# Low parts of the MLP weights from an adding DMA instead of VectorE, in a float32 two-layer trunk

## The chip, the cores and the metric

The kernel runs on one core of one Trainium2 chip. The metric is the device time of one execution, in microseconds. A core has TensorE (PE, matmuls; PEld is its weight load), VectorE (DVE), ScalarE (ACT), GpSimd (POOL), SyncE (SP) and 16 DMA engines that all queues share.

## The reference

One sequence of 256 tokens with 2048 features goes through two layers, each with attention, a layer norm, an MLP of 8192 hidden features and another layer norm. The change touches the MLPs alone:

```
def sq_relu_mlp(x, w1, w2):
    return jnp.square(jax.nn.relu(x @ w1)) @ w2
...
h = layer_norm(ALPHA * h + mix, ln1_g[layer], ln1_b[layer])
h = layer_norm(ALPHA * h + sq_relu_mlp(h, mlp_w1[layer], mlp_w2[layer]), ln2_g[layer], ln2_b[layer])
```

Layer 0 has a causal attention with forget gates, layer 1 an attention over compressed, selected and windowed keys. All inputs are float32; `w1` is 2048 x 8192 and `w2` 8192 x 2048 a layer.

## The kernel before

Every large product is made from float32r parts: a float32 operand x is split into a high part (x rounded to float32r) and a low part (x minus high), and a product takes three of the four combinations: high x high, high x low, low x high.

Weights come in blocks of 128 partitions x 1024 float32, 512 KB, "half k" of a block of weights. `wload` makes one ready: a load into one of 4 `raw` buffers, issued on SP's DMA queue, then `fill_split`, in which ScalarE rounds `raw` to the high half of a `whl` tile (L117) and VectorE subtracts the high half from `raw` into the low half of the tile (L118). There are 5 `whl` buffers. ScalarE can start when a `whl` buffer has been released by the matmuls that read it and the load has landed; the `raw` buffer comes free when VectorE is done, and the SP queue then issues the load of the block four later. The queues of all engines work in order.

`mlp(layer, acts, ln)` goes through the hidden features in four quarters of 2048. In a quarter, the w1 stage (`ws_stream`, `ws_many`) takes 16 slices of 128 columns of w1, each in two halves of 8 row blocks. A row block kt needs two matmuls: a wide one with the high weights against both halves of the activations (L151, 512 columns) and a low one with the low weights against the high activations (L152, 256 columns). So a half has 16 matmuls. In the first quarter the first three slices run together. Each finished slice is merged (ScalarE L185, VectorE L187), squared behind its relu (VectorE L385) and split into an activation chunk. The w2 stage (`out_proj`, `xs_part`, `xs_mm`) takes 512 output columns at a time (index n) over four parts kc of 512 hidden features, each part in two halves of the weights (index k); a half has 12 matmuls of 512 columns (L173): per row block and 128 tokens high x high, high activations x low weights, low x high. The last quarter leaves its last 512 columns to `end`, which calls `wload` itself and overlaps the layer norm.

GpSimd issues a few DMAs in the attention layers: four of 512 KB into the tile `bc`, four into `nbm`, one of 2 MB into `b_dram`, and small ones. In the MLPs it has nothing to do until the last layer norm. `warm` is a run of matmuls without use, put into the norms.

Of the kernel before, what the change touches and what calls it, by code (L numbers as in the profile page):

```python
# [52 lines left out]
def constants():  # L53
    """Identity, triangles, stacked identities and masks: they depend on shapes alone."""
    i = np.arange(P)
    eye = np.eye(P, dtype=np.float32)
    upper = (i[:, None] <= i[None, :]).astype(np.float32)
    causal = np.where(i[None, :] > i[:, None], np.float32(BIG), np.float32(0))

    def stacked(n):  # L60
        a = np.zeros((P, n), np.float32)
        a[np.arange(2 * n), np.arange(2 * n) % n] = 1
        return a

    t = np.arange(S).reshape(2, P)
    d_c = t[:, :, None] - (16 * np.arange(NC) + 31)
    keep = (d_c >= 0).astype(np.float32).transpose(1, 0, 2).reshape(P, 2 * NC)
    cst = [eye, upper, np.ones((P, P), np.float32), np.zeros((P, P), np.float32), causal,
           stacked(60), stacked(48), stacked(16), keep]

    def onehot(*dists):
        """Block k of 32 rows picks the bucket of distance k; row 96 + k says that the key lies ahead."""
        a = np.zeros((99, len(dists[0])), np.float32)
        c = np.arange(len(dists[0]))
        for k, dist in enumerate(dists):
            ok = dist >= 0
            a[NB * k + buckets(dist)[ok], c[ok]] = -1
            a[96 + k, c[~ok]] = 1
        return a

    oh = [onehot(255 - np.arange(384))]
    for tb in range(2):
        oh += [onehot(*(d_c[tb, :, n + k] for k in range(3))) for n in range(0, NC, 3)]
    ahead = np.zeros((99, 3, H), np.float32)
    ahead[[96, 97, 98], [0, 1, 2]] = BIG
    oh.append(ahead.reshape(99, 3 * H))
    return np.ascontiguousarray(np.concatenate(cst, 1)), np.ascontiguousarray(np.concatenate(oh, 1))
# [11 lines left out]
def _trunk(nc, tc, i, out, ctx):  # L99
# [23 lines left out]
    def wload(src, k, pool=wp, bufs=5, pieces=1):  # L123
        """Half k of a block of weights, split."""
        raw = raw_tile()
        w = pool.tile([P, 2, HALF], F32R, tag="whl", name="whl", bufs=bufs)
        n = HALF // pieces
        for s in (slice(a, a + n) for a in range(0, HALF, n)):
            load(raw[:, s], src[k][:, s])
            fill_split(w[:, 0, s], w[:, 1, s], raw[:, s])  # L130
        return w

# [8 lines left out]

    def ws_many(srcs, acts, accs, half=None):
        """accs = (128 columns of a matrix each)^T @ x^T, over the wide halves of x; half: rows 0-1023 or the rest."""
        for kt in range(KT) if half is None else range(8 * half, 8 * half + 8):
            if kt % 8 == 0:
                ws = [wload(src, kt // 8) for src in srcs]
            a = acts[kt // 4][:, kt % 4]
            s = slice(kt % 8 * P, (kt % 8 + 1) * P)
            last = kt == KT - 1
            for w, acc in zip(ws, accs):  # L150
                wide = lambda: mm(acc, w[:, 0, s], a, start=kt == 0, stop=last)  # L151
                low = lambda: mm(acc[:, :S], w[:, 1, s], a[:, 0, :], start=False, stop=False)  # L152
                if last:
                    low(), wide()
                else:
                    wide(), low()

    def ws_stream(srcs, acts, use, together=1):
        """Each of srcs is one 128-column slice of a matrix; use(j, acc) gets its product, transposed."""
        j = 0  # L160
        while j < len(srcs):
            n = together if j == 0 else 1
            accs = [acc_tile() for _ in range(n)]
            ws_many(srcs[j:j + n], acts, accs)
            for k, acc in enumerate(accs):
                use(j + k, acc)
            j += n
# [6 lines left out]

    def xs_part(src, act, accs, first, last, pieces=1):
        """accs[t] += (512 columns of x)[tokens t] @ 512 x 512 of a matrix"""
        ws = [wload(src, k, pieces=pieces if k == 0 else 1) for k in range(2)]
        for kt in range(4):
            for t in range(2):
                xs_mm(accs[t], act, kt, t, ws[kt // 2], first and kt == 0, last and kt == 3)  # L180

    def merge(dst, acc, scale=1.0):
        """dst = scale * (the wide product's two halves)"""
        t = sp.tile([P, S], F32, tag="mt", name="mt")
# [6 lines left out]
    def narrow(src, n, acts, st, dst):  # L191
        """dst[:, tok, :] = x @ (2048 x n) for a small n; returns its last step."""
        raw = wp.tile([P, KT, n], F32, tag="raw", name="nraw", bufs=4)
# [31 lines left out]

    def out_proj(src, acts, first, ln=None, two=False, between=()):
        """h = (ALPHA h or h) + acts @ W, 512 columns at a time (two: the first 1024 at once).

        between's steps come after the parts. With ln, the last 512 columns are left to what it returns,
        which ends with the layer norm."""  # L230
        between = list(between)
# [13 lines left out]
        def one(n, accs, kcs):  # L245
            for kc in kcs:
                xs_part(src[n, kc], acts[kc], accs[n], kc == 0, kc == 3)
                step()
# [19 lines left out]
        def end(late, meanwhile=None):  # L268
            """Tokens 128-255 come behind, so that the norm of the others overlaps with their products."""
            ln.gains(late)  # L270
# [30 lines left out]
    class Norm:  # L301
        """Layer norm of h in place, in pieces of 128 tokens x 512 features, with what use does to a piece."""

# [55 lines left out]
    def transposer(cs):  # L359
        """Puts the pieces into cs, transposed and split, in chunks of 512 features."""  # L360
        def use(t, c):
# [14 lines left out]
    def mlp(layer, acts, ln):  # L376
        for q in range(4):
# [9 lines left out]

            ws_stream([i["w1"][layer, q * 16 + j] for j in range(16)], acts, use, 3 if q == 0 else 1)
            end = out_proj(i["w2"][layer, q], hid, q == 0, ln if q == 3 else None)
        with tc.tile_pool(name="late", bufs=2) as late:  # L390
            end(late)

    # ---- attention: the steps that both kinds share
    def exp_rows(E, L, m, sums):
# [4 lines left out]

    # ================= layer 0: forgetting attention  # L400
    bfb = cp.tile([P, H], F32, name="bfb")
# [8 lines left out]
    def warm(n, lhs, rhs):  # L410
        """Keeps the tensor engine's clock up while it waits."""
        idle = ps_lg.tile([P, 512], F32, tag="lg", name="idle")
# [18 lines left out]
    def forget_gates():  # L431
        """Log of the forget gates."""
        f = sp.tile([P, 5, 2, H], F32, name="f", bufs=1)
# [144 lines left out]
    with tc.tile_pool(name="late", bufs=2) as late:  # L578
# [6 lines left out]
        def tables():  # L585
            """Tables of the relative bias, negated, with BIG where a key lies ahead"""
            r_ps = ps_lg.tile([P, 512], F32, tag="lg", name="rps")
# [17 lines left out]

    # ================= layer 1: sparse attention over keys and values of layer 0's output
    with tc.tile_pool(name="np", bufs=2) as np_:
# [4 lines left out]
        gate = np_.tile([P, 2, 3 * H], F32, name="gate", bufs=1)  # L612
        # keys of the two branches and of the compressed blocks, split: per group, high and low parts of
        # [selected 0-127, window 0-127, compressed, selected 128-255, window 128-255]
        kT = np_.tile([P, G, 2, KW], F32R, name="kT", bufs=1)
        kcT = np_.tile([P, G, NC], F32, name="kcT", bufs=1)
        vhl = np_.tile([P, 2, 2, 512], F32R, name="vhl", bufs=1)
        v1 = np_.tile([P, 2, 512], F32, name="v1", bufs=1)
        # compressed values in three bands of rows (high, high, low parts), to meet high, low and high weights
        vc = np_.tile([BAND, G, P], F32R, name="vc", bufs=1)  # L620
# [5 lines left out]
        def bands(t):  # L626
            """The three bands of the columns of t"""
            return bass.AP(tensor=t.tensor, offset=t.offset, ap=[*[list(x) for x in t.ap[:-1]], [32, 3], [1, NC]])
# [46 lines left out]
        def compress(s):  # L675
            """First product of the compression; returns its later steps."""
            acc = acc_tile()
# [180 lines left out]
def laid_out(a):  # L858
    """The inputs in the order in which the kernel reads them."""
    def cols(w):  # L860
        # 128 columns of all rows, in two halves of the rows: [n, half, p, (kt c)]
        k, n = w.shape
        return w.reshape(2, k // P // 2, P, n // P, P).transpose(3, 0, 2, 1, 4).reshape(n // P, 2, P, HALF)

    def rows(w):
        # 512 columns of 512 rows, in two halves of the rows: [n, kc, half, p, (kt c)]
        k, n = w.shape
# [53 lines left out]
```

## Time and profile before

| | |
|---|---|
| time, median of 2 runs | 2260.77 us (2259.89 to 2261.65) |
| span of the profiled execution, first to last instruction | 2258.3 us |
| around that span, against the median | 2.5 us |
| mean granted TensorE clock | 0.995 of full speed |
| TensorE busy | 2233.2 us, 99% |
| VectorE busy | 1406.5 us, 62% |
| ScalarE busy | 1047.0 us, 46% |
| GpSimd busy | 18.5 us, 1% |
| DMA, all queues | 427.54 MB, mean 189 GB/s |
| SP's queue | 419.00 MB, 56.9% of 16 engines' time |

Busy time does not count the issue of DMAs, and a busy TensorE is not one at its peak, because its matmuls are pipelined. The share of DMA is the time that packets took on the 16 engines. An engine's idle time matters only where the chain of work that ended last goes through it.

### The profile page before, as it was taken

What the parts mean: (1) busy time and instruction counts of PE and PEld (TensorE: products, weight loads), DVE (VectorE), ACT (ScalarE), POOL (GpSimd) and SP (SyncE); (2) the same over time, 40 slices, a digit from 0 to 9 for tenths busy, and PEclk for the clock granted to TensorE, in tenths of its full rate; (3) what the DMA queues carried; (4) which work ended last, traced back from release to release, by engine and by line L of the source; (5) the groups of instructions that cost most, each with busy time, mean ns of one, the idle gap of its engine ahead of it and who ended that gap; (6) DMA issues with size and microseconds to landing.
All of it is one profiled execution on the core that took longest, in us unless ns stands there. A gap on an engine that the chain in (4) does not pass through costs nothing.

```text
span 2258.3 us, 30147 instructions
## 1 busy us (share of the span) xinstructions
PE 2233.2 (99%) x11478; PEld 1890.7 (84%) x11478; DVE 1406.5 (62%) x2209; ACT 1047.0 (46%) x1564; POOL 18.5 (1%) x26
## 2 busy tenths in 40 slices
PE   9999999999999999999999999999999999999997
PEld 7888888888888888888788888888888888888885
DVE  6565556764565565565786688667655645655655
ACT  5444444443444444444355567544434434444442
POOL 0000000000000000000000000000000000000001
PEclk9999999999999999999999999999999999999998
DMA  7665557556555555555556744565565566565563
GB/s 252 197 206 180 173 197 243 195 187 191 191 186 192 192 187 191 191 187 190 183 170 211 252 134 133 171 212 177 187 194 188 187 194 189 186 195 188 187 194 113
DMA packets 116829, 427.54 MB, mean 189 GB/s; under 512 B 13179, under 2 KB 13339, under 8 KB 115406
## 3 DMA queue, kind: packets, MB, share of 16 engines
q1 hardware_dynamic: 114734, 419.00, 56.9%
q0 software_dynamic: 1952, 6.63, 1.0%
q8 instruction: 90, 1.47, 0.3%
q14 instruction: 53, 0.43, 0.1%
HBM read 423.45 MB, written 4.24 MB: 189 GB/s over the span
## 4 chain that ended last, share of the span: by engine, by line
PE 97%; DVE 2%; DMA 1%; ACT 0%; issue 0%; SPq 0%; DVEq 0%
PE acc L173 44%; PE acc L151 31%; PE acc L152 16%; PE acc L683 1%; PE pt L367 1%; PE pt L830 1%; PE pt L808 0%; PE lg L766 0%; DMA bc<-c_dram 0%; DVE h L354 0%; PE acc L199 0%; PE pt L831 0%; PE pt L524 0%; PE lg L491 0%; PE lg L762 0%; DVE h L339 0%
## 5 line engine op out<-in xcount | busy, mean ns | idle before, releaser
L118 DVE TENSOR_TENSOR whl<-raw,whl 128x1024 fp32r<-128x1024 f32 (+1 forms) x769 | 937.9, 1223 | 617.9 <-ACT whl L117 608.5
L117 ACT CAST whl<-raw 128x1024 fp32r<-128x1024 f32 (+1 forms) x769 | 804.5, 1049 | 740.4 <-PE acc L173 489.6
L151 PE MATMUL acc<-act,whl 128*128 128x512 f32 x3072 | 1089.5, 401 | 0.0
L173 PE MATMUL acc<-whl,act 128*128 128x512 f32 x4416 | 1011.7, 390 | 1.0 <-DVE whl L118 1.0
L173 PEld LDWEIGHTS acc<-whl,act 128*128 128x128 f32 x4416 | 827.6, 188 | 175.4 <-DVE whl L118 1.8
L152 PE MATMUL acc<-act,whl 128*128 128x256 f32 x3072 | 834.3, 282 | 0.0
L151 PEld LDWEIGHTS acc<-act,whl 128*128 128x128 f32 x3072 | 569.7, 189 | 124.1 <-issue 0.2
L152 PEld LDWEIGHTS acc<-act,whl 128*128 128x128 f32 x3072 | 581.4, 189 | 16.7
L185 ACT ACTIVATE mt<-acc 128x256 f32<-128x256 f32 x192 | 73.3, 382 | 308.6 <-PE acc L151 308.6
L187 DVE TENSOR_TENSOR mu<-acc,mt 128x256 f32<-128x256 f32 x128 | 54.1, 424 | 120.3 <-ACT mt L185 120.3
L385 DVE SCALAR_TENSOR_TENSOR mu<-mu 128x256 f32<-128x256 f32 x128 | 54.2, 425 | 4.2
L117 ACT CAST act<-mu 128x256 fp32r<-128x256 f32 x128 | 52.0, 408 | 4.3 <-DVE mu L385 2.6
L118 DVE TENSOR_TENSOR act<-mu,act 128x256 fp32r<-128x256 f32 x128 | 53.4, 419 | 0.0
L117 ACT CAST act<-pt 128x256 fp32r<-128x256 f32 x80 | 29.5, 372 | 43.8 <-PE pt L367 32.7
L241 DVE TENSOR_TENSOR h<-h,acc 128x512 f32<-128x512 f32 x48 | 30.8, 681 | 13.2 <-PE acc L173 13.2
L118 DVE TENSOR_TENSOR act<-pt,act 128x256 fp32r<-128x256 f32 x80 | 33.0, 419 | 9.2 <-ACT act L117 9.0
L395 ACT ACTIVATE E<-E,sm 128x128 f32<-128x128 f32 (+1 forms) x64 | 29.0, 453 | 7.7 <-DVE sm L398 7.4
L354 DVE SCALAR_TENSOR_TENSOR h<-h,mv,lnb 128x256 f32<-128x256 f32 (+1 forms) x53 | 26.5, 541 | 0.1
L395 ACT ACTIVATE E<-L,sm 128x128 f32<-128x128 f32 (+1 forms) x32 | 14.3, 449 | 25.3 <-DVE sm L398 25.3
L367 PE MATMUL pt<-cst,h 128*128 128x128 f32 x96 | 18.8, 294 | 6.3 <-DVE h L354 6.0
L339 DVE SCALAR_TENSOR_TENSOR h<-h,mv,lng 128x256 f32<-128x256 f32 (+1 forms) x53 | 25.0, 501 | 0.0
L239 DVE SCALAR_TENSOR_TENSOR h<-h,acc 128x512 f32<-128x512 f32 x32 | 20.6, 680 | 4.5 <-PE acc L173 4.5
(173 smaller groups left out, 664.9 us busy)
## 6 DMA issues: line engine op xcount, KB each, us to landing
raw<-in_w SPq DMA_DIRECT2D x512, 512.0 KB, 3.5
raw<-in_fq SPq DMA_DIRECT2D x32, 512.0 KB, 3.6
raw<-in_fk SPq DMA_DIRECT2D x32, 512.0 KB, 3.5
raw<-in_fo SPq DMA_DIRECT2D x32, 512.0 KB, 3.6
raw<-in_kvT SPq DMA_DIRECT2D x32, 512.0 KB, 4.4
raw<-in_nq SPq DMA_DIRECT2D x32, 512.0 KB, 3.6
raw<-in_no SPq DMA_DIRECT2D x32, 512.0 KB, 3.6
raw<-in_fv SPq DMA_DIRECT2D x31, 512.0 KB, 3.5
```

The lines of the kernel that those rows point to most:

```text
L117: nc.scalar.copy(hi, src)
L118: nc.vector.tensor_sub(lo, src, hi.bitcast(F32))
L151: wide = lambda: mm(acc, w[:, 0, s], a, start=kt == 0, stop=last)
L152: low = lambda: mm(acc[:, :S], w[:, 1, s], a[:, 0, :], start=False, stop=False)
L173: mm(acc, l, w[:, r, s], start=first and n == 0, stop=last and n == 2)
L185: nc.scalar.activation(t, acc[:, S:], AF.Copy, scale=scale)
L187: nc.vector.tensor_add(dst, acc[:, :S], t)
L241: nc.vector.tensor_add(hcols(t, n), hcols(t, n), acc)
L354: nc.vector.scalar_tensor_tensor(hs, hs, rstd, b, op0=OP.mult, op1=OP.add)
L367: nc.tensor.transpose(tp[:, k * P:(k + 1) * P], h[:, t, f:f + P], eye)
L385: nc.vector.scalar_tensor_tensor(u, u, 0.0, u, op0=OP.max, op1=OP.mult)
L395: nc.scalar.activation(E, L, AF.Exp, bias=m, scale=-1.0, accum_out=sums)
```

## The change

A new function `wload_added` makes some of the blocks ready in another way. ScalarE writes the high half as before, and then, in a second pass over `raw`, the negated rounded value into the low half; a DMA issued by GpSimd adds `raw` onto that low half in place, which leaves raw minus high. VectorE has no part in it. The source of the adding DMA is the `raw` buffer (`far` False) or once more the weights in DRAM (`far` True).

In w1 it is used for the second half (kt 8 to 15) of each slice, except for the slices that run together; the source is `raw`. In w2 it is used for the second half of the parts kc 1 and 3, except in `end`; the source is DRAM. The other blocks, the attention layers and the numbers of buffers stay as they are. (The docstrings and comments that the diff also takes out are left out here.)

```diff
+    def wload_added(src, k, far):
+
+        raw = raw_tile()
+        w = wp.tile([P, 2, HALF], F32R, tag="whl", name="whl", bufs=5)
+        load(raw, src[k])
+        nc.scalar.copy(w[:, 0, :], raw)
+        nc.scalar.mul(w[:, 1, :], raw, -1.0)
+        nc.gpsimd.dma_start(w[:, 1, :], src[k] if far else raw, accum_op=OP.add)
+        return w
+
...
-    def ws_many(srcs, acts, accs, half=None):
+    def ws_many(srcs, acts, accs, half=None, added=False):
...
-                ws = [wload(src, kt // 8) for src in srcs]
+                ws = [wload_added(src, 1, False) if added and kt else wload(src, kt // 8) for src in srcs]
...
-    def ws_stream(srcs, acts, use, together=1):
+    def ws_stream(srcs, acts, use, together=1, added=False):
...
-            ws_many(srcs[j:j + n], acts, accs)
+            ws_many(srcs[j:j + n], acts, accs, added=added and j >= together)
...
-    def xs_part(src, act, accs, first, last, pieces=1):
+    def xs_part(src, act, accs, first, last, pieces=1, added=False):
...
-        ws = [wload(src, k, pieces=pieces if k == 0 else 1) for k in range(2)]
+        ws = [wload_added(src, k, True) if added and k else wload(src, k, pieces=pieces if k == 0 else 1) for k in range(2)]
...
-    def out_proj(src, acts, first, ln=None, two=False, between=()):
+    def out_proj(src, acts, first, ln=None, two=False, between=(), added=False):
...
-                xs_part(src[n, kc], acts[kc], accs[n], kc == 0, kc == 3)
+                xs_part(src[n, kc], acts[kc], accs[n], kc == 0, kc == 3, added=added and kc % 2 == 1)
...
-            ws_stream([i["w1"][layer, q * 16 + j] for j in range(16)], acts, use, 3 if q == 0 else 1)
-            end = out_proj(i["w2"][layer, q], hid, q == 0, ln if q == 3 else None)
+            ws_stream([i["w1"][layer, q * 16 + j] for j in range(16)], acts, use, 3 if q == 0 else 1, True)
+            end = out_proj(i["w2"][layer, q], hid, q == 0, ln if q == 3 else None, added=True)
```

## Rows read from the trace of the kernel before

**Rows 1.** The page, its parts 1 and 4: busy time and share of the span of each engine, and the shares of the chain of work that ended last.

```profile
PE 2233.2 (99%) x11478; PEld 1890.7 (84%) x11478; DVE 1406.5 (62%) x2209; ACT 1047.0 (46%) x1564; POOL 18.5 (1%) x26
...
PE 97%; DVE 2%; DMA 1%; ACT 0%; issue 0%; SPq 0%; DVEq 0%
```

**Rows 2.** The page, its part 5, groups by line over the whole run: line, engine, operation, out<-in, count | busy us, mean ns of one | idle us of the engine just before them, and who ended most of it.

```profile
L118 DVE TENSOR_TENSOR whl<-raw,whl 128x1024 fp32r<-128x1024 f32 (+1 forms) x769 | 937.9, 1223 | 617.9 <-ACT whl L117 608.5
...
L117 ACT CAST whl<-raw 128x1024 fp32r<-128x1024 f32 (+1 forms) x769 | 804.5, 1049 | 740.4 <-PE acc L173 489.6
...
L151 PE MATMUL acc<-act,whl 128*128 128x512 f32 x3072 | 1089.5, 401 | 0.0
...
L173 PE MATMUL acc<-whl,act 128*128 128x512 f32 x4416 | 1011.7, 390 | 1.0 <-DVE whl L118 1.0
```

**Rows 3.** Busy time by windows, core 0, a w2 stage (677 to 766 us) and a w1 stage (766 to 854 us) of the first MLP.

```profile
core 0: us, PE busy (x) PEld busy (x) DVE busy (x) ACT busy (x) POOL busy (x), PEclk, DMA share, GB/s
677.00:766.00 89.00, 89.00 (x397) 73.82 (x396) 45.67 (x44) 35.39 (x35) 0.00 (x0) 1.00 0.60 193
766.00:854.00 88.00, 88.00 (x500) 76.31 (x499) 55.97 (x77) 42.82 (x62) 0.00 (x0) 1.00 0.58 186
```

**Rows 4.** The timeline of ScalarE in a w1 stage: start us, duration us, engine, line, operation, out<-in, count [idle before <- releaser].

```profile
596.06 1.05 ACT L117 CAST whl<-raw 128x1024 fp32r<-128x1024 f32 x1 [1.12 <-PE acc L152]
598.85 0.38 ACT L185 ACTIVATE mt<-acc 128x256 f32<-128x256 f32 x1 [1.74 <-PE acc L151]
599.13 1.04 ACT L117 CAST whl<-raw 128x1024 fp32r<-128x1024 f32 x1
600.18 0.41 ACT L117 CAST act<-mu 128x256 fp32r<-128x256 f32 x1
601.71 1.05 ACT L117 CAST whl<-raw 128x1024 fp32r<-128x1024 f32 x1 [1.12 <-PE acc L152]
...
607.36 1.05 ACT L117 CAST whl<-raw 128x1024 fp32r<-128x1024 f32 x1 [1.06 <-PE acc L152]
```

**Rows 5.** Who waited for whom between 595 and 680 us (w1): us in total, times, longest.

```profile
ACT mt L185 <- PE acc L151: 27.0, 15, 1.8
...
ACT whl L117 <- PE acc L152: 16.0, 15, 1.1
```

**Rows 6.** The timelines of VectorE and of SP's DMA queue in the same stage, columns as in rows 4.

```profile
597.14 1.22 DVE L118 TENSOR_TENSOR whl<-raw,whl 128x1024 fp32r<-128x1024 f32 x1 [1.03 <-ACT whl L117]
...
598.39 0.33 SPq L114 DMA_DIRECT2D raw<-in_w  x1
```

**Rows 7.** DMA between 595 and 680 us (w1): the hardware queue (packets, MB, share of 16 engines' time), the loads (count, KB each, median us from issue to landing), and the spread of that time.

```profile
q1 hardware_dynamic: 4322, 15.74, 57.8%
...
raw<-in_w SPq DMA_DIRECT2D x30, 512.0 KB, 3.5
...
DMA to landing us min/median/max: 3.3/3.5/3.8
```

**Rows 8.** The timeline of ScalarE in a w2 stage, columns as in rows 4.

```profile
519.55 1.05 ACT L117 CAST whl<-raw 128x1024 fp32r<-128x1024 f32 x1 [1.67 <-PE acc L173]
522.27 1.06 ACT L117 CAST whl<-raw 128x1024 fp32r<-128x1024 f32 x1 [1.67 <-PE acc L173]
```

**Rows 9.** The DMAs of 512 KB that GpSimd issues in the attention layers, from DRAM into the tiles `bc` and `nbm`: duration of the issue in ns (min/median/max), first and last start, and the time from issue to landing.

```profile
L469 POOL DMA_DIRECT2D bc<-c_dram x4: 527/530/559, 47.4 to 131.2; - x4
...
DMA to landing us min/median/max: 4.6/5.3/5.9
...
L750 POOL DMA_DIRECT2D nbm<-b_dram x4: 748/752/766, 1140.8 to 1400.7; - x4
...
DMA to landing us min/median/max: 4.1/4.2/6.0
```

**Rows 10.** The DMA issues of the whole run: the largest transfer of GpSimd, DRAM to DRAM: engine, count, KB, us from issue to landing.

```profile
b_dram<-r_dram POOLq DMA_DIRECT2D x1, 2048.0 KB, 9.7
```

**Rows 11.** DMA between 500 and 590 us (w2), the same three lines as in rows 7.

```profile
q1 hardware_dynamic: 4776, 17.36, 60.6%
...
raw<-in_w SPq DMA_DIRECT2D x34, 512.0 KB, 4.2
...
DMA to landing us min/median/max: 3.4/4.2/4.6
```

**Rows 12.** DMA between 40 and 140 us, where GpSimd's four `bc` transfers run beside loads of weights: the software queue (packets, MB, share of 16 engines' time).

```profile
q0 software_dynamic: 608, 2.11, 7.5%
```

**Rows 13.** Busy time by windows, two stretches in which TensorE waits (columns as in rows 3; PEclk is the granted clock as a share of full speed).

```profile
60.00:70.00 10.00, 8.85 (x52) 7.50 (x51) 9.07 (x22) 4.24 (x9) 0.53 (x1) 1.00 0.65 222
...
400.00:410.00 10.00, 7.21 (x36) 5.96 (x36) 8.21 (x25) 2.06 (x6) 1.32 (x2) 0.66 0.62 204
```

## The prediction

> **What bounds the kernel now.** I read the totals first, then the chain of work that ended last: TensorE is busy 99% of the span, the chain is 97% PE, and VectorE holds 2% of it [rows 1]. The groups by line say the same from the other side: over the whole run the matmuls that read weight blocks waited 1.0 us for a VectorE split, while VectorE and ScalarE sat idle in front of their splits for 618 and 740 us [rows 2]. The windows by stage confirm it for the MLPs: in a w1 and in a w2 stage PE is busy in every microsecond, VectorE about 51 to 64% [rows 3]. So the change takes work from an engine that ends nothing. What matters is how early a block of weights is ready, and the timelines tell that.
>
> The w1 pace: the splits of the odd halves start at 596.06, 601.71 and 607.36 [rows 4], so one column slice (two blocks) takes PE 5.65 us, a block 2.83 and a pair of slices 11.30. The even halves (599.13) start behind the merge. Every odd split is released by PE [rows 4, 5]: a `whl` buffer coming free starts it, its data have long been there. VectorE starts 0.03 us after ScalarE's part and ends at 598.36, and the next load into that `raw` buffer is issued at 598.39 [rows 6]; it lands 3.5 us later, at 601.9, 5.5 us before its split at 607.36 [rows 7]. That 5.5 us is the cover on which the change draws. In w2 the pace is 2.72 us a half [rows 8].
>
> **What is removed, added and moved.** In w1 the second half of each column slice is changed, except for the first three slices of a layer's first quarter: 13+16+16+16 = 61 a layer, 122 in all. In w2 it is only the second half of parts kc 1 and 3, two of eight halves: 15 column blocks x 2 = 30 a layer, 60 in all. So 182 of the 512 MLP loads are changed, 36% and not half.
>
> VectorE loses 182 x 1.223 us = 223 us [rows 2]. None of it was on the path: worth 0. ScalarE gets a second pass over `raw`: I price it like the first, 1.05 us, 191 us in all. In w1 it starts where ScalarE now sits idle for 1.74 us ahead of the merge [rows 4], in w2 in a gap of 1.67 us [rows 8]: it costs no ScalarE queueing, only delay of the block. Without that gap the merge and the next split behind it would come up to 1.05 us later.
>
> GpSimd gets 182 DMA issues; one of 512 KB holds its queue 0.53 to 0.75 us [rows 9]. Nothing else is queued there inside the MLPs. The SP queue has as many loads as before, but in w1 a load into an odd `raw` buffer now waits for the add to land, not for VectorE, because the add reads `raw`; all later loads stand behind it in SP's order. In w2 the add reads DRAM again, so `raw` comes free after ScalarE's second pass, at about the time of today.
>
> **The add itself** is in no row, so I bound it. Call X its time from issue to landing. Plain copies of 512 KB from GpSimd's queue land in 4.1 to 6.0 us, medians 4.2 and 5.3 [rows 9]; the slowest landing from that queue, of 2 MB, is 9.7 us [rows 10]. Nearest are the 5.3 us copies, which ran beside loads. An add must fetch two operands for one result, so I add the engine time of one more plain transfer: 57.8% of 85 us over 30 loads = 1.64 us [rows 7]. X = 5.3 + 1.64 = 6.9 us, with 4.1 and 9.7 as ends. A gain is excluded, since PE waited 1.0 us for splits in all [rows 2].
>
> **w1, the raw loop.** There are 4 `raw` buffers and two blocks a slice, so two of the four buffers always hold changed halves, and each must go round in 11.30 us: two ScalarE passes 2.1, hand-overs about 0.1 (0.03 each [rows 6]), X, then the next load L. With today's L of 3.5 the loop closes if X is at most 11.3 - 5.7 = 5.6 us. With adds on the same engines L will not stay 3.5: at a DMA share of 60.6% it is already 4.2, at most 4.6 [rows 11]. I take 4.2. Loop = 2.1 + 0.1 + 6.9 + 4.2 = 13.3 us, 2.0 us more than PE needs for a pair.
>
> The engine time gives a second view. Four loads a pair take 4 x 1.64 = 6.6 us. GpSimd's copies took 7.5% of 100 us for 2.11 MB, 1.86 us per 512 KB [rows 12]; two adds at that price make 10.3 us a pair (fits), at twice that 14.0 us (2.7 us over). The loop's 13.3 lies between; it is my value.
>
> The excess must first eat the lead. An odd block gets its buffer at 596.0, its add would land at 598.2 + 6.9 = 605.1, and PE needs it four blocks after the release, at 607.3: 2.2 us in hand, regained in each w2 stage, so 8 x 2.2 = 18 us are free. w1 costs 61 pairs x 2.0 - 18 = **+104 us**.
>
> **w2.** Same reckoning: release 519.5, add landed at 519.55 + 2.2 + 6.9 = 528.7, wanted at 519.5 + 4 x 2.72 = 530.4. Cover 1.7 us: 0, as long as X stays under 8.6; beyond, 60 times the excess. Engine time for four halves: 4 x 1.60 [rows 11] + 3.72 = 10.1 of 10.9 us, just inside.
>
> The sum: the profiled execution's span of 2258.3 us and 2.5 us around it make 2260.8, the median of the two runs; +104 gives **2365 us**, +4.6%.
>
> One rule of the Trainium skill bears on X. Collectives: The Full Stack, section "The bandwidth ceiling: the fold count and why AG ≠ RS ≠ AR", has the adding transfer at half the rate of a copy because it reads two sources, the add costing nothing, with about 31 GB/s per engine for the copy. By its figures 16 engines would add 512 KB in an estimated 2.1 us and a pair would need 6.6 + 4.2 = 10.8 us, inside 11.3, which is the first rival. No run here shows an adding transfer yet.
>
> **The rivals.** *No change, the other side*: the add is little dearer than GpSimd's copies, X at most 5.6 us with L near 3.5. Then the raw loop closes in 11.3 us, PE never waits, and the time is 2261. For it: medians of 4.2 and 5.3 us [rows 9]. Against: the same rows go up to 6.0 for plain copies, and loads slow down with the share. If X ends between 5.6 and 6.6 with L at 3.5, the loss stays under 45 us (1.0 x 61, less 8 x 2.5 us of lead), also no change by what a measurement of this kernel can tell, 2%. Chance 0.24.
>
> *Much dearer adds*: X = 9.7, L = 4.6. Loop 16.5, +5.2 x 61 = 317; no lead is left, and w2 loses (9.7 - 8.6) x 60 = 66: 2644. For it: the two reads and the write of one byte range may not overlap as a copy's do; no row excludes it. TensorE's clock could add to it: the granted clock was 0.66, between 1.2 and 2.4 GHz, in a stretch with PE idle 2.8 of 10 us, but 1.00 with 1.15 of 10 idle [rows 13]; my forecast idles 2.0 of 13.3, between these. Chance 0.12.
>
> *The change doesn't do what it says*: a third of the blocks, and 191 us of the 223 us return on ScalarE. That gives 2261 too and is counted with no change. *Faster*: a less busy VectorE could shorten the norms, whose share of the chain is part of those 2%, but the change leaves their instructions alone: 0.02 over 2%.
>
> **How the numbers follow.** My forecast's mechanism holds 0.62, with 2306 to 2547 as its own range: 2306 is X = 6.6 with L = 3.5, where the loss is no longer told from none, and the top is X = 9.0 with L = 4.4 (loop 15.6, +4.3 x 61 = 262, no lead left, w2 0.4 x 60 = 24: 2547). No change reaches down to 2257. So the range is 2257 to 2547; it leaves out the dear adds and the faster case, some 0.14. Faster 0.02, same 0.24, slower 0.74.
>
> **What would show it.** Right: idle PE in the w1 stages ahead of the low matmuls (L152), released by the adding DMA; odd loads waiting for that DMA in SP's waits; landing of the add near 7 us; w1 slices at about 6.6 us in place of 5.65; w2 stages still 32 x 2.72 = 87 us; DMA share in w1 near 90%. Wrong: adds landing within 5.6 us and slices at 5.65 (no change), or waits in w2 as well (dear adds). If ScalarE's second pass is not 1.05 us, or the adds do not overlap with one another on GpSimd's queue, the loop's terms are off by that much.

## The result and the profile after

The changed kernel takes 2293.9 us, median of 2 runs (2290.3 and 2297.5), against 2260.8 before: 1.0145 times as long, interval 1.0126 to 1.0164. That is 33 us more; the prediction had 104. The time lies inside the prediction's whole range (2257 to 2547), whose lower part comes from the rival of no change, and under its mechanism's own (2306 to 2547). The profiled execution has a span of 2288.4 us, 30 us more than before.

The page of the changed kernel: busy time by engine, the DMA queues (packets, MB, share of 16 engines' time), the chain that ended last by engine, the groups by line that changed, and the DMA issues (count, KB, median us from issue to landing). Lines from 132 on stand 10 lower than before: L161 and L162 are the wide and low matmuls of w1, L183 those of w2, L138 and L139 ScalarE's two passes, L140 the adding DMA.

```profile
PE 2242.8 (98%) x11478; PEld 1893.5 (83%) x11478; DVE 1197.3 (52%) x2033; ACT 1211.7 (53%) x1740; POOL 170.1 (7%) x202
...
q1 hardware_dynamic: 114734, 419.00, 55.3%
q0 software_dynamic: 27296, 98.92, 23.0%
...
PE 83%; DMA 11%; DVE 2%; issue 2%; ACT 1%; SPq 0%; POOLq 0%; ACTq 0%; POOL 0%; DVEq 0%
...
L118 DVE TENSOR_TENSOR whl<-raw,whl 128x1024 fp32r<-128x1024 f32 (+1 forms) x593 | 722.6, 1222 | 598.4 <-ACT whl L117 592.9
...
L162 PE MATMUL acc<-act,whl 128*128 128x256 f32 x3072 | 837.8, 283 | 13.6 <-DMA whl<-raw 12.8
...
L139 ACT ACTIVATE whl<-raw 128x1024 fp32r<-128x1024 f32 x176 | 185.7, 1055 | 0.0
...
L140 POOL DMA_DIRECT2D whl<-raw x116 | 99.7, 860 | 766.8 <-ACT whl L139 471.2
L140 POOL DMA_DIRECT2D whl<-in_w x60 | 51.8, 863 | 602.4 <-ACT whl L139 551.0
...
raw<-in_w SPq DMA_DIRECT2D x512, 512.0 KB, 5.1
whl<-raw POOLq DMA_DIRECT2D x116, 512.0 KB, 6.6
whl<-in_w POOLq DMA_DIRECT2D x60, 512.0 KB, 7.9
```

VectorE lost 209 us, ScalarE gained 165, and PE now waits 12.8 us for the add from `raw` (before: 1.0 us for splits in all [rows 2]). The chain has 11% of DMA in it. So the kind of loss is the forecast one, and the add's own time is nearly the forecast one; the size is not.

A w1 stage away from the first quarter shows why that is odd. DMA between 590 and 680 us, then the timeline of ScalarE, GpSimd and SP's queue around three changed halves (the line with x6 stands for six loads, the last of which is the one at 617.16):

```profile
q1 hardware_dynamic: 4428, 16.12, 49.7%
q0 software_dynamic: 2160, 7.87, 47.3%
```

```profile
608.08 1.05 ACT L138 CAST whl<-raw 128x1024 fp32r<-128x1024 f32 x1 [1.12 <-PE acc L162]
...
613.74 1.05 ACT L138 CAST whl<-raw 128x1024 fp32r<-128x1024 f32 x1 [1.12 <-PE acc L162]
614.69 1.06 ACT L139 ACTIVATE whl<-raw 128x1024 fp32r<-128x1024 f32 x1
...
619.39 1.05 ACT L138 CAST whl<-raw 128x1024 fp32r<-128x1024 f32 x1 [0.66 <-PE acc L162]
...
610.38 0.86 POOL L140 DMA_DIRECT2D whl<-raw  x1 [4.83 <-ACT whl L139]
616.04 0.86 POOL L140 DMA_DIRECT2D whl<-raw  x1 [4.79 <-ACT whl L139]
...
601.95 15.54 SPq L114 DMA_DIRECT2D raw<-in_w  x6
...
617.16 0.33 SPq L114 DMA_DIRECT2D raw<-in_w  x1
```

The second pass ends at 615.75 and the add is issued 0.29 us later. The DMA engines are at 97% of their time, loads land in 5.1 us and adds in 6.6, so a buffer's turn is 2.0 + 0.3 + 6.6 + 5.1 = 14.0 us, longer than the forecast's 13.3. Yet the odd splits start 5.65 us apart, as before [rows 4]. Where the time went is told by the start of the first matmul of each stage, in the trace of a kernel, less that in the trace of before; the table gives what each stage added to it, in us (q0 to q3 are the quarters; the first quarters are counted from behind the norm, and the attention layers are left out).

```
                    layer 0                                layer 1
              w1q0 w2q0 w1q1 w2q1 w1q2 w2q2 w1q3 w2q3 | w1q0 w2q0 w1q1 w2q1 w1q2 w2q2 w1q3 w2q3
changed       10.9  0.9  0.0  0.1  1.9  0.0  0.0  1.2 |  9.9  0.0  1.2  0.5  2.1  0.0  0.0  0.0
e3 (turns)    18.0  5.6 12.0  5.0 13.8  3.5 14.6  6.5 | 16.6  5.0 12.3  7.4 13.9  5.9 14.0  4.2
e5 (DRAM)      7.2  0.6  1.3  0.0  0.0  0.0  0.6  0.0 |  4.1  0.7  0.0  0.0 -0.1  0.6  0.1  0.0
e6 (more raw)  7.0  0.0  0.0  0.0  0.0  0.0  0.0  4.4 |  2.6  0.0  0.0  0.0  0.0  0.0  0.0  4.1
e7 (not q0)   -0.1  0.9  1.0  0.8  0.0  0.4  0.0  0.0 |  0.0  0.0  0.0  0.0  2.7  1.3 -0.1  0.1
e8 (copy)      5.1  0.0  0.0  0.0  0.0  0.0  0.0  0.0 |  5.6  0.0  0.0  0.0  0.0  0.0  0.0  0.0
e9 (gains)     8.3  0.7  0.9  0.1  0.0  0.0  0.0  4.9 |  4.7  0.0  0.0  0.3  1.4  1.4  0.0  4.4
e12 (q0 only) 10.9  0.0  0.0  0.0  0.0  0.0  0.0  0.0 |  8.9  0.0  0.0  0.0  0.0  0.0  0.0  0.0
e13 (slice 8)  1.2  1.1  0.0  0.0  1.9  1.2  2.6  1.6 |  1.6  1.1  0.0  0.0  0.7  1.8  0.2  1.2
```

Of the 29 us by which the changed kernel's last matmul starts later, 20.8 fall in w1 of the two first quarters; in the six others w1 loses 0 to 2.1 us each. The rows e3 to e13 belong to the experiments below.

### The profile page after: what moved, and what is told of

The parts are those of the page before. It is cut to its first block, busy times and chain, and to the rows that moved or that the text cites. A ratio compares the mean times of both kernels' runs of the same rounds, so it can differ in the third digit from the quotient of the medians.

```text
span 2288.4 us, 30658 instructions
## 1 busy us (share of the span) xinstructions
PE 2242.8 (98%) x11478; PEld 1893.5 (83%) x11478; DVE 1197.3 (52%) x2033; ACT 1211.7 (53%) x1740; POOL 170.1 (7%) x202
## 4 chain that ended last, share of the span: by engine, by line
PE 83%; DMA 11%; DVE 2%; issue 2%; ACT 1%; SPq 0%; POOLq 0%; ACTq 0%; POOL 0%; DVEq 0%
PE acc L183 42%; PE acc L161 24%; PE acc L162 12%; DMA raw<-in_w 5%; DMA whl<-raw 4%; DMA whl<-in_w 1%; DVE whl L118 1%; ACT whl L117 1%; PE pt L840 1%; PE pt L818 0%; PE lg L776 0%; DMA bc<-c_dram 0%; PE pt L377 0%; DVE h L364 0%; PE acc L693 0%
## 5 line engine op out<-in xcount | busy, mean ns | idle before, releaser
L161 PE MATMUL acc<-act,whl 128*128 128x512 f32 x3072 | 1093.9, 402 | 3.1 <-ACT whl L117 3.1
L118 DVE TENSOR_TENSOR whl<-raw,whl 128x1024 fp32r<-128x1024 f32 (+1 forms) x593 | 722.6, 1222 | 598.4 <-ACT whl L117 592.9
L183 PE MATMUL acc<-whl,act 128*128 128x512 f32 x4416 | 1012.8, 390 | 3.8 <-DMA whl<-in_w 1.7
L183 PEld LDWEIGHTS acc<-whl,act 128*128 128x128 f32 x4416 | 826.9, 188 | 180.0 <-DMA whl<-in_w 3.1
L117 ACT CAST whl<-raw 128x1024 fp32r<-128x1024 f32 (+1 forms) x593 | 620.6, 1049 | 540.5 <-PE acc L183 300.9
L162 PE MATMUL acc<-act,whl 128*128 128x256 f32 x3072 | 837.8, 283 | 13.6 <-DMA whl<-raw 12.8
L161 PEld LDWEIGHTS acc<-act,whl 128*128 128x128 f32 x3072 | 571.8, 189 | 127.1 <-ACT whl L117 3.5
L162 PEld LDWEIGHTS acc<-act,whl 128*128 128x128 f32 x3072 | 583.5, 190 | 35.3 <-DMA whl<-raw 17.0
L138 ACT CAST whl<-raw 128x1024 fp32r<-128x1024 f32 x176 | 185.1, 1052 | 209.1 <-PE acc L183 96.6
L139 ACT ACTIVATE whl<-raw 128x1024 fp32r<-128x1024 f32 x176 | 185.7, 1055 | 0.0
L140 POOL DMA_DIRECT2D whl<-raw x116 | 99.7, 860 | 766.8 <-ACT whl L139 471.2
L140 POOL DMA_DIRECT2D whl<-in_w x60 | 51.8, 863 | 602.4 <-ACT whl L139 551.0
```

What stands on the lines that cost most here:

```text
L117: nc.scalar.copy(hi, src)
L118: nc.vector.tensor_sub(lo, src, hi.bitcast(F32))
L138: nc.scalar.copy(w[:, 0, :], raw)
L139: nc.scalar.mul(w[:, 1, :], raw, -1.0)
L140: nc.gpsimd.dma_start(w[:, 1, :], src[k] if far else raw, accum_op=OP.add)
L183: mm(acc, l, w[:, r, s], start=first and n == 0, stop=last and n == 2)
```

## The experiments

Theory A: the turns of the `raw` buffers decide, and the prediction had these turns wrong. The addresses in the compiled program show them: `raw` buffers are not handed round in a fixed order. In the steady w1 stages the buffer of a changed half is given out again 5 blocks later, that of a plain half 3 blocks later. The trace agrees: the half that is loaded at 601.95 has its first pass at 608.08 and its add at 610.38, and when that add has landed, at 617.1, the load at 617.16 starts, the fifth behind it. A turn then has 5 x 2.83 = 14.1 us for the 14.0 us of a changed half and 8.5 us for the 2.3 + 5.1 = 7.4 us of a plain one: it just closes. Theory B: the time of the DMA engines decides, 97% used.

**Fixed turns.** The four buffers are split in two and two, so that a changed half's buffer comes round every 4 blocks, as the prediction assumed.

```diff
-    def raw_tile():
-        return wp.tile([P, HALF], F32, tag="raw", name="raw", bufs=4)
+    def raw_tile(odd=0):
+        return wp.tile([P, HALF], F32, tag="raw%d" % odd, name="raw%d" % odd, bufs=2)
...
-        raw = raw_tile()
+        raw = raw_tile(k % 2)
```

> The changed kernel, but with the four raw buffers split into two for first halves and two for second halves of weight blocks, so that a buffer of a changed half comes round every 4 blocks as the prediction assumed (in the changed kernel it is given every 5 blocks and a plain half's every 3). Theory A (the raw buffers' turns decide): with add 6.5 us, load 5.1, two passes 2.1 and the issue 0.3 behind them a turn takes 14.0 us against 11.3, or 13.3 if the loads get quicker again; w1 slows to 6.6 to 7.0 us a slice and the kernel to about 2360 (2330 to 2400). Theory B (the DMA engines' time decides, the turns don't): as the changed kernel, 2294.

Measured 2427.5 us, 1.0746 (1.0724 to 1.0767), +167 us: above A's range, and far from B. The timeline of ScalarE in the second quarter, with the first passes of four changed halves running, PE's waits over the whole run (us, times, longest), and one line of what SP's queue waited for between 640 and 700 us:

```profile
623.13 1.05 ACT L138 CAST whl<-raw 128x1024 fp32r<-128x1024 f32 x1 [1.72 <-PE acc L162]
...
629.33 1.05 ACT L138 CAST whl<-raw 128x1024 fp32r<-128x1024 f32 x1 [1.62 <-DMA raw<-in_w]
...
637.34 1.05 ACT L138 CAST whl<-raw 128x1024 fp32r<-128x1024 f32 x1 [3.98 <-PE acc L161]
...
642.58 1.05 ACT L138 CAST whl<-raw 128x1024 fp32r<-128x1024 f32 x1 [1.60 <-DMA raw<-in_w]
```

```profile
PE acc L162 <- DMA whl<-raw: 86.0, 68, 3.4
PE acc L183 <- DMA whl<-in_w: 27.7, 9, 4.3
```

```profile
SPq L114 <- DMA whl<-raw: 26.8, 8, 5.0
```

A slice takes (642.58 - 623.13) / 3 = 6.5 us, and the w1 stages of the table lose 115 us over 116 adds, 2.0 us a pair: the prediction's own loop, in the turns it had assumed. (The compiled program of this run differs in one thing more: in w1 SP's queue loads the plain half of the next slice ahead of the changed half of this one. It waits for an add all the same, 8 times between 640 and 700 us.) w2 loses 43 us more, which the prediction had at 0; its stages follow w1 stages that have used up every lead, which is argued and not traced.

The control keeps the fixed turns and takes the adds out:

> The kernel before with the raw buffers split in two and two, no adds: the control for the fixed turns. A plain half holds its buffer 2.3 us of splitting and 3.5 to 4.2 us of loading in a turn of 11.3 us: no loss, 2258 to 2264. If it loses, the fixed turns themselves cost, not the adds in them.

2266.8 us, 1.0029 (1.0020 to 1.0039): a miss by some 3 us, but its trace loses nothing from the first MLP on. The 9 us by which it comes late are there at the start of the first MLP, in layer 0's attention. So the MLP losses of the experiment come from adds in fixed turns. (The order of loads that came with them is not in the control, whose w1 loads, but for the first ones of the first quarters, stand in the order of the source.)

**More buffers.** The changed halves of w1 get three `raw` buffers of their own, in a pool beside.

```diff
+        raw = raw_tile() if far else more[-1].tile([P, HALF], F32, tag="mraw", name="mraw", bufs=3)
```

> The changed kernel, but the changed halves of w1 load into three raw buffers of their own (a turn of 6 blocks, 17 us) beside the four of the others. The DMA work is the same. Theory A (turns of the raw buffers): the waits in the first quarter of each MLP go almost wholly, 2262 to 2272. Theory B (DMA engines at 97% in w1): no change against the changed kernel, 2290 to 2297.

2279.2 us, 1.0082 (1.0067 to 1.0097). Between the theories: 14 of the 33 us go with the DMA work unchanged, which B excludes (the order of the loads in SP's queue changed with the buffers); 19 stay, more than A said. By the table all w1 loss behind the first quarters is gone, and the first quarters still lose 7.0 and 2.6 us; there the DMA engines are nearly full. Windows of that kernel (busy us by engine, granted clock, DMA share, GB/s):

```profile
440.00:470.00 30.00, 25.52 (x133) 21.93 (x132) 11.79 (x22) 18.46 (x27) 4.27 (x5) 0.89 0.92 263
470.00:500.00 30.00, 30.00 (x171) 26.00 (x171) 13.30 (x22) 19.37 (x27) 4.30 (x5) 1.00 1.01 277
```

That full engines are what stops it there is not shown, and the second window speaks against it: at a share of 1.01 PE is busy throughout. The 4 us in the last w2 stage of each MLP are new, and were not followed up.

**Adds of w1 from DRAM.** The `raw` buffer comes free after the second pass.

```diff
-                ws = [wload_added(src, 1, False) if added and kt else wload(src, kt // 8) for src in srcs]
+                ws = [wload_added(src, 1, True) if added and kt else wload(src, kt // 8) for src in srcs]
```

> The changed kernel, but the adds of w1 also read the weights from DRAM again, so that the raw buffer comes free after ScalarE's second pass; 116 x 0.52 MB more are read from DRAM, the adds themselves are as many. Theory A (turns of the raw buffers): faster than the changed kernel, 2265 to 2280, unless adds land later than 8.7 us, where the whl buffers are late. Theory B (DMA time): the same or slower than the changed kernel, 2294 to 2310.

2275.9 us, 1.0065 (1.0048 to 1.0083), inside A's range: adds that land later (8.0 us) and move more from DRAM cost half as much, as theory A has it: they don't hold `raw`. The first quarters still lose 7.2 and 4.1 us.

**Where the adds stand.** First w1 or w2 alone, by leaving `added` off in the other stage:

> Adds in w1 alone (116), w2 as in the kernel before. Theory A: the waits of w1 stay, 2283 to 2290 (in the trace of the changed kernel w1 stages lost 10.9 + 9.9 + 1.9 + 1.2 + 2.1 us against the kernel before). Theory B (DMA time): w2 no longer takes DMA time, part of the lead is rebuilt in w2; 2275 to 2290.

> Adds in w2 alone (60, from DRAM), w1 as in the kernel before. The prediction's cover for w2 was 1.7 us with the add at 6.9 us; it landed at 7.9, still under 8.6. All theories: 2261 to 2265, at most 0.2%.

2286.3 us, 1.0115 (1.0100 to 1.0130), and 2260.6 us, 1.0001 (0.9992 to 1.0011). The adds of w1 carry the loss; those of w2 alone are free, though they land at 7.9 us: the cover reckoned for w2 holds. Beside the adds of w1 they are perhaps not free: with both, the time is 2293.9 us against 2286.3 with w1's alone, but the intervals overlap. Both theories' ranges had room for 2286. Then the first quarters:

```diff
-            ws_stream([i["w1"][layer, q * 16 + j] for j in range(16)], acts, use, 3 if q == 0 else 1, True)
+            ws_stream([i["w1"][layer, q * 16 + j] for j in range(16)], acts, use, 3 if q == 0 else 1, q > 0)
```

> The changed kernel, but w1 of the first quarter of each MLP is left as in the kernel before (26 adds fewer of 176). Theory A (the loss arises where no lead of ready blocks exists and cannot be built up, right behind a norm): 20 of the 33 us go, 2268 to 2276. Rival (each add costs its share): 33 x 26/176 = 5 us go, 2289. Theory B (DMA time) lies near the rival.

2267.7 us, 1.0030 (1.0016 to 1.0044): 26 of the 33 us go with 26 of 176 adds. And the other way round, `q == 0` and no adds in w2:

> Adds only in w1 of the first quarter of each MLP, 26 in all. Theory A: these 26 carry most of the loss, +15 to +21 us, 2276 to 2282. Rival (the adds of the quarter before leave engines or buffers behind, the loss needs all 176): 2261 to 2266.

2278.7 us, 1.0088 (1.0073 to 1.0103): these 26 adds alone cost 18 us, and by the table they cost it in the stages in which they stand.

**What is the matter with the first quarter.** Windows of 12 us in the first one, one line of the kernel before and then the changed kernel:

```profile
432.00:444.00 12.00, 12.00 (x69) 10.42 (x68) 9.74 (x14) 5.61 (x9) 0.00 (x0) 1.00 0.81 267
```

```profile
432.00:444.00 12.00, 8.06 (x34) 6.06 (x33) 3.12 (x4) 4.26 (x6) 0.85 (x1) 0.80 0.86 243
444.00:456.00 12.00, 12.00 (x64) 10.24 (x64) 5.73 (x10) 7.62 (x11) 1.70 (x2) 0.92 0.82 229
456.00:468.00 12.00, 11.79 (x68) 10.06 (x67) 5.16 (x9) 8.08 (x12) 1.71 (x2) 1.00 0.97 278
...
480.00:492.00 12.00, 10.64 (x61) 9.01 (x60) 5.45 (x9) 7.98 (x13) 1.72 (x2) 1.00 0.98 266
```

Some 25 us into the stage, where the three slices that run together are done and the changed halves begin, PE stands still for 3.9 of 12 us, and the granted clock falls to 0.80 and 0.92; then it goes on waiting a little. The chain through it is a plain half (start, us, what):

```profile
432.64 1.23 DVE whl L118
433.89 5.07 DMA raw<-in_w
439.06 1.05 ACT whl L117
440.13 1.24 DVE whl L118
```

A load is issued the moment a split frees its buffer and is wanted the moment it lands: no lead.

In layer 0 this wait has a second cause, which the compiled program shows: PE's instructions there do not stand in the order of the source. The plain halves of slices 3 to 6 come first, with a single matmul of each changed half between them, and the other 15 matmuls of each of these changed halves only behind the last plain one. So PE uses up plain halves faster than one a slice, and waits for one while work on changed halves stands behind it (two of their adds, issued at 422.22 and 431.05, have landed by 437.8). The buffers are not given out 5 and 3 blocks later there: the plain half of slice 6 gets the buffer that the plain half of slice 5 has just left, which is the chain above, and the changed half of slice 6 gets it next. PE around the wait, and its waits between 407 and 512 us:

```profile
436.61 0.40 PE L161 MATMUL acc<-act,whl 128*128 128x512 f32 x1
440.16 0.79 PE L161 MATMUL acc<-act,whl 128*128 128x512 f32 x1 [3.15 <-ACT whl L117]
...
441.80 0.63 PE L161 MATMUL acc<-act,whl 128*128 128x512 f32 x1
...
442.44 0.63 PE L161 MATMUL acc<-act,whl 128*128 128x512 f32 x1
...
450.36 0.40 PE L161 MATMUL acc<-act,whl 128*128 128x512 f32 x1
...
450.72 0.40 PE L161 MATMUL acc<-act,whl 128*128 128x512 f32 x1
```

```profile
PE acc L161 <- ACT whl L117: 3.1, 1, 3.1
PE acc L162 <- DMA whl<-raw: 2.5, 5, 1.4
```

In layer 1's first quarter (1546 to 1649 us) the program keeps the order of the source, and PE's waits are all for adds:

```profile
PE acc L162 <- DMA whl<-raw: 6.0, 4, 2.4
```

There 9.9 us are lost all the same, so the loss does not hang on that order; how much of layer 0's 10.9 us it costs was not separated.

SP's queue gave another thought. In it the load of `lng` waits 17.0 us ahead of the w1 loads (`SPq L114 <- DVE h L364: 17.0, 1, 17.0`), so I thought that this wait emptied the lead, and put the gains' loads behind the last w2 loads:

```diff
-            ln.gains(late)
+            with tc.issue_after(queue[-1]):
+                ln.gains(late)
```

> The changed kernel, but the loads of the MLP norm's gains (lng and lnb, 1 MB each) are put behind the last w2 loads in SP's order. In both kernels lng stands in SP's queue ahead of w1 loads of the first quarter and waits 17 us there for its buffer. Theory A': that wait empties the lead of ready blocks just where the changed halves begin, and the changed kernel can't rebuild it; then the first-quarter loss (10.9 + 9.9 us) falls to some 2 us each, 2268 to 2276. Rival (the norm itself or the three slices that run together at the start empty the lead): 2287 to 2294.

2287.1 us, 1.0124 (1.0106 to 1.0143), in the rival's range. That theory fell: the first quarters still lose 8.3 and 4.7 us, and the late gains cost 4.9 and 4.4 us at the ends of w2. With the `raw` buffers full, SP's loads had to wait anyway: in this run one waits 30.1 us for a VectorE split. Whether the norm or the three slices that run together empty the lead was not tried. Both edits together:

> Both edits: gains' loads later, and three raw buffers of their own for the changed halves of w1. Theory A': nearly no loss is left but for waits at the end of w2's last quarter (4 us each with more raw buffers alone), 2261 to 2270. Rival (DMA engines at 97 to 100% of their time in w1): 2276 or more.

2280.0 us, 1.0086 (1.0071 to 1.0101), as with the buffers alone, and in the rival's range. That does not show full engines to be the cause, for the reason given there.

What was left of theory A was that the lead is missing behind the norm and is not built up again. In the changed kernel four buffers give a block every (14.0 + 7.4) / 2 / 4 = 2.68 us, 0.15 us ahead of PE a block; before, every (2.3 + 3.5) / 4 = 1.45 us. So I let the changed halves begin at slice 8 of the first quarter and not at slice 3:

> The changed kernel, but in the first quarter of each MLP the changed halves begin with slice 8 in place of slice 3 (10 adds fewer of 176). Theory A: behind the norm PE has hardly a ready block in hand; with plain halves the lead is rebuilt in five slices, with changed halves it is not, since the raw buffers' turns give a block every (14.0 + 7.4)/2/4 = 2.68 us against 2.83 us that PE needs. Then most of the first-quarter loss goes, as where the whole quarter is left plain: 2267 to 2274. Rival (the first quarter is dear all along, whatever stands before the adds): 8/13 of its 21 us stay, 2283 to 2290.

2276.2 us, 1.0064 (1.0047 to 1.0081), 2 us above A's range and outside the rival's. The table is clearer: the two first quarters lose 1.2 and 1.6 us in place of 10.9 and 9.9. In layer 0 this edit also brings PE's program nearly back to the order of the source, so there two things changed; layer 1, in that order in both kernels, shows what the later start alone does. The windows of this run in the first quarter:

```profile
410.00:440.00 30.00, 29.91 (x180) 26.03 (x179) 25.06 (x50) 16.19 (x30) 0.00 (x0) 1.00 0.60 209
440.00:470.00 30.00, 30.00 (x173) 26.16 (x172) 14.90 (x23) 17.88 (x25) 3.50 (x4) 1.00 0.79 215
470.00:510.00 40.00, 39.07 (x210) 33.03 (x209) 18.05 (x27) 22.93 (x31) 4.29 (x5) 1.00 0.96 276
```

Its other stages lose 13 us in small pieces, more than in the changed kernel (8); with turns that just close, where these fall differs from run to run and was not traced.

**The price of the parts.** ScalarE's second pass without the DMA, with VectorE subtracting as before:

```diff
-        nc.gpsimd.dma_start(w[:, 1, :], src[k] if far else raw, accum_op=OP.add)
+        nc.vector.tensor_sub(w[:, 1, :], raw, w[:, 0, :].bitcast(F32))
```

> ScalarE's second pass over raw stays in the 176 halves, but VectorE then writes the low half by subtraction as before, and there is no adding DMA. Theories A and B: nothing, 2259 to 2263. Rival (ScalarE's 185 us are part of the loss, because its merges and splits come later): 2270 to 2290.

2260.9 us, 1.0004 (0.9995 to 1.0014): free. And a copy for the add (`accum_op` left out):

> The DMA of the 176 halves copies raw over the low half in place of adding to it (this leaves out the subtraction, so the low half holds the raw weights). The number of DMAs and the bytes from the source are the same, one operand less. If an add's second operand is what it costs over a copy: landing of the copy near 5 us instead of 6.6, share of the software queue in a w1 stage about 23% instead of 45%, loads back at 4 us, time 2261 to 2268. If the issue on GpSimd's queue or the waits around it are the cost: 2285 to 2294.

2276.0 us, 1.0067 (1.0052 to 1.0082): a miss, half of the loss stays without the second operand. DMA between 590 and 680 us:

```profile
q1 hardware_dynamic: 4372, 15.94, 56.5%
q0 software_dynamic: 2160, 7.87, 24.1%
...
raw<-in_w SPq DMA_DIRECT2D x31, 512.0 KB, 4.4
whl<-raw POOLq DMA_DIRECT2D x15, 512.0 KB, 4.2
```

The engine time of a copy is 24.1% of 90 us over 15, 1.45 us, that of an add 47.3% over 15, 2.84 us. But a copy, too, holds `raw` until it has landed (5.4 us median over the run), and the first quarters, where no lead is in hand, lose 10.7 us to it; no other stage of the MLPs loses anything.

## Why the prediction was right or wrong

- **What bounds the kernel, and what the removed and moved work is worth: right.** VectorE's 209 us less and ScalarE's 186 us of second passes are worth nothing either way: the second pass alone measured 1.0004, and the 60 halves of w2 without VectorE's split, with the second pass and the add in its place, 1.0001.
- **The count: slightly wrong.** The first slice of the later quarters also stays plain (j must be at least `together`, which is 1 there): 58 changed halves of w1 a layer and not 61, 176 in all.
- **X: right.** 6.9 us forecast, 6.6 measured from `raw`, 7.9 from DRAM. Its parts came near as well: a copy in the add's place lands in 5.4 us (5.3 taken), so the second operand costs 1.2 (1.64 taken). **L: too small**, 4.2 against 5.1, and the 0.3 us until GpSimd's issue was counted as 0.1. By these alone the forecast loss would have been larger. The second view, by engine time, had 10.3 to 14.0 us a pair; 97% of 11.3 us, 11.0, was measured.
- **The raw loop: the step that failed.** "Two of the four buffers always hold changed halves, and each must go round in 11.30 us" took the buffers to be handed round in turn. The compiled program gives them out again 5 blocks after a changed half and 3 after a plain one, so the loop has 14.1 us and the steady w1 stages lose next to nothing. With the turns forced to 4 blocks the loss per pair was 2.0 us, as reckoned. The sound test would have been the mean hold of a buffer against 4 x 2.83 us: (14.0 + 7.4) / 2 = 10.7 against 11.3.
- **The lead of 18 us taken off the sum: not borne out.** The prediction gave each w1 stage 2.2 us in hand at its start. In the first quarters the changed halves begin with no lead, and there 20.8 of the 29 us were lost; with the turns forced to 4 blocks w1 lost all of 58 x 2.0 us, with nothing taken off.
- **The number.** The 33 us are not a smaller part of the forecast 104: the steady loop, which was to give them all, gave next to none, and most of what was measured arose where the sum had put a gain. That the time came out inside the whole range is owed to the rival.
- **w2: right** for w2 alone (1.0001). Behind w1 stages in forced turns w2 lost 43 us, which the prediction had at 0.
- **The rivals.** "No change" had the reason wrong (X at most 5.6 us) and came close in size: the loss lies inside the 2% up to which a measurement of this kernel counts as no change, although its interval (1.0126 to 1.0164) leaves no doubt that there is a loss. "Dearer adds" did not come. TensorE's clock did fall where PE stood still, to 0.80 in one window, which is part of the first quarter's loss: a wide and a low matmul took 0.64 us together after the wait, 0.36 later.
- **What would show it:** of the marks named, PE's waits for the add, the landing near 7 us and the share near 90% (97%) came; slices of 6.6 us did not. The slices were the one mark of the loop itself; the others only say that adds are there and land late.

## What to carry to other kernels

When a change makes some blocks hold a buffer longer, compare the mean hold of all blocks with the buffers times the pace, and look up in the compiled program how buffers are really handed out, and in which order the instructions stand, before giving any of them a fixed turn; an experiment's edit can change both. A pipeline that just closes at its pace costs nothing in the steady state and much wherever it begins empty, so look at each place where the lead is gone (behind a norm, at a change of stage) for itself. To take work off an engine that ends nothing gained nothing here, and what replaced that work used up such leads.

## What the runs showed of the hardware

- An adding DMA of 512 KB from SBUF takes 2.84 us of engine time against 1.45 us for the copy in its place, 1.96 times as much. The ratio is a rough one: the two stretches differ in share (97% and 81%), and a load took 1.46 us in the one and 1.67 in the other (56.5% of 90 us over 15.94 MB). The rule of the Trainium skill that the prediction weighed (Collectives: The Full Stack, "The bandwidth ceiling: the fold count and why AG ≠ RS ≠ AR": half the rate, because two sources are read; the page states it for the reduce step of a ring) agrees in the ratio; the 2.1 us estimated from its figures was too low.
- The engine time of a load is not a fixed price: it took 1.64 us at a share of 58% [rows 7] and, by 49.7% of 90 us over 16.12 MB, 1.46 us per 512 KB at 97%. So a share of 97% did not mean that the pace was lost.
- GpSimd's queue is held 0.86 us by the issue of an add, against 0.53 to 0.75 us for copies before [rows 9].
- The granted clock was 0.80 in the 12 us in which PE stood still for 3.9 us, and 0.92 in the next 12, in which PE was busy throughout. Behind the wait of 3.15 us in the first of them a wide and a low matmul took 0.64 us together (441.80 to 442.44), and 0.36 us later on (450.36 to 450.72).
